# One hybrid encoder block on one core: the input projection's matmuls ordered by part, and the FFN's casts, closing tiles and stores queued anew

## The chip, the cores and the metric

The kernel runs on one core of a Trainium2 chip. The metric is the device time of one execution in microseconds (us); the value before is the median of three runs. A profile of one further execution is read beside it. TensorE (PE) multiplies, ScalarE (ACT) and VectorE (DVE) cast, add and evict, GpSimd (POOL) does small reductions and issues some of the DMAs, and SyncE (SP) issues most of the others. PEld is the row of TensorE's weight loads.

## What is computed

The input is x of 1 x 2048 x 1024 in float32. The layer, cut to what matters:

```python
h = rms_norm(x, pre_mix_g)
proj = h @ w_in                                   # 1024 -> 5376 columns
p_att, p_rwkv, p_gate = split(proj)               # 1536, 1792, 2048 columns
y_a = chunk_band_attention(q, k, v, rel_bias)     # own chunk of 64 and 8 before it
y_b = rwkv7_time_mix(p_rwkv, ...)                 # token shift, decay, delta rule over time
merged = sigmoid(ga) * (y_a @ proj_a) + sigmoid(gb) * (y_b @ proj_b)
x = x + rms_norm(merged @ w_out, post_mix_g)
hf = rms_norm(x, pre_ffn_g)
u = square(relu(hf @ w_up)) @ w_down              # 1024 -> 4096 -> 1024
x = x + rms_norm(u, post_ffn_g)
```

## The kernel before

**Precision.** Every large product is made of three matmuls. An operand is split into a high part, rounded to a short format by a cast on ACT (L78), and a low part, the rest, made by a subtraction on DVE (L79). `mm3` (L82) then adds high x high, high x low and low x high in one PSUM bank. It can go through the contraction block by block, three matmuls for each, or, with its last argument, by part: all high x high, then all high x low, and the low weights last.

**Mixing.** The 2048 tokens are worked on in four groups of 512. A group goes through `phase_rwkv`, `phase_attention` and `phase_merge`. In the first two stand 42 blocks of the input projection, each a call of `dense` (L108) for 128 columns: a load of 512 KB into `wraw` (two buffers), the cast to `whi` on ACT and the subtraction to `wlo` on DVE (two buffers each), 24 matmuls of 128x128 on 128x512 into a bank `psd` (two banks), and an eviction by whoever called. Sixteen of the blocks are gates (`gate`, L743), which ACT evicts (L747) and stores. The gates have no other dependence, and they are strewn between the steps of the RWKV recurrence (ST, L702, on DVE and PE) and of a triangular inverse that runs on DVE for some 30 us at a time (L584, L590). In the kernel before, only the first two blocks of the program multiply by part; the other 166 go by contraction block.

**The order of instructions.** Nothing of the order on an engine is fixed by the program text alone. A planner goes through the instructions with estimated costs; on each engine it places next the one that it believes ready, and among those the one that comes first in the program. On the chip each engine then works its queue strictly in the planned order. `queue_behind(a, b)` (L92) puts a into the queue after b without a semaphore, `keep_in_program_order` pins an instruction, and `place` (L96) hangs some matmuls of the recurrence behind the n-th matmul of the projection.

**FFN.** The hidden layer is worked on in two halves of 1024 tokens, with a seven-product scheme for 2x2 blocks (additions on DVE take the place of an eighth product). `phase_up` (L1226) makes the products of w_up. For each of 16 pairs of column blocks it loads two `wraw` (four buffers) and splits the combinations a1, s12, s3 and s4. The first eight (`early`) have their A11 product made ahead of the loop, so that the loop begins to load and split a1 at i = 8. The results X are squared relus, evicted by DVE and ACT (L1278 to L1280) and stored on POOL's queue to `xd`.

`phase_down` (L1347) multiplies them with w_down in 56 steps: seven products, named 1, 6, 7, 5, 4, 3, 2 in this order, of eight steps each. A step loads `xraw` and `wdraw` (L1378 to L1383), splits both into one operand tile `fop` and makes 24 matmuls; the last two steps of a product are taken together. Operands are prepared two steps ahead. After a product's last step `gather` (L1406) adds its banks to u. The closing tile of 128 tokens, `final` (L1418), loads x1 (L1422), sums squares on ACT (L1427), scales on DVE (L1428), takes the root on POOL (L1430, L125, L127), adds on DVE (L1434) and stores the output on SP's queue (L1437). The first four closing tiles stand behind product 4, the other four behind products 3 and 2.

**Beside it.** While the first half's `phase_down` runs, a generator `beside` (L1515) does work for the second half: a residual and its transposes, combinations of h on POOL's queue, and `first_half(2)` (L1217), which loads four pieces of h, casts each on ACT (L1214) and subtracts on DVE (L1215) in place.

## Time and profile before

| what | value |
|---|---|
| median of 3 runs | 3273.53 us (3273.09 to 3274.3) |
| profiled execution, its own time | 3273.41 us |
| its span, first to last instruction | 3271.7 us |
| mean granted TensorE clock | 0.996 |
| ACT busy | 1571.1 us (48%) |
| DVE busy | 2244.4 us (69%) |
| POOL busy | 592.7 us (18%) |
| one cast of 128x1024 on ACT (whi) | 1.05 us |
| one subtraction of 128x1024 on DVE (wlo) | 1.23 us |

"Idle before" in a group's row, and the bracket behind a row of the timeline, is the time that the engine stood still ahead of these instructions, with what ended it. Matmuls are pipelined: each is shown for some 0.39 us while they follow each other at shorter steps, so that a small delay can vanish in the overlap. A window's row gives a stretch, its length, each engine's busy time with the count of instructions in it, the granted clock as a share of full speed, the DMA engines' share and GB/s. A row of the timeline that ends in xN is a run of N like instructions.

### The profile page before, as it was taken

To read this page: it belongs to the slowest core of one execution; us is meant where nothing else is said; L and a number is where in the kernel's file an instruction comes from. 1 tells how busy PE (TensorE), PEld (TensorE's weight loads), DVE (VectorE), ACT (ScalarE), POOL (GpSimd) and SP (SyncE) were. 2 spreads that over 40 slices of the span, in tenths; PEclk is the share of its full clock that TensorE was granted. 3 is DMA by queue.
4 is the path that set the end of the run, shared out by engine and by line. 5 is a ranking of instruction groups with operands and counts; after the bars stand their busy time and mean duration, and the time that the engine had idled before them with its cause. 6 is when DMAs were issued, how large, how long until landed. Compare 5 with 4: busy or idle time off the path is not lost. (4 is left out here: it accounts for less than half of the span.)

```text
span 3271.7 us, 49957 instructions
## 1 busy us (share of the span) xinstructions
PE 3178.6 (97%) x18913; PEld 2591.9 (79%) x18913; DVE 2244.4 (69%) x3655; ACT 1571.1 (48%) x2511; POOL 592.7 (18%) x1093
## 2 busy tenths in 40 slices
PE   8999999999999999999999999999999999999998
PEld 6777778777878777878777877878888877888887
DVE  7785666776766775776876775777655768775465
ACT  4434634444644434644434754444543444444333
POOL 2221013122112222102222110121211112120000
PEclk9999999999999999999999999999999999999999
DMA  5245373247574237565336557654787875556565
GB/s 167 85 137 175 121 241 119 72 147 245 172 227 133 88 111 246 182 207 164 94 97 225 165 183 256 196 184 149 263 280 251 281 240 185 167 177 228 193 213 180
DMA packets 432282, 592.53 MB, mean 181 GB/s; under 512 B 25301, under 2 KB 295841, under 8 KB 432041
## 3 DMA queue, kind: packets, MB, share of 16 engines
q1 hardware_dynamic: 375080, 413.14, 40.4%
q0 software_dynamic: 47744, 159.42, 13.3%
q10 hardware_dynamic: 9216, 16.78, 1.4%
q8 instruction: 149, 2.44, 0.3%
q14 instruction: 93, 0.75, 0.1%
HBM read 425.37 MB, written 167.01 MB: 181 GB/s over the span
## 5 line engine op out<-in xcount | busy, mean ns | idle before, releaser
L1401 PE MATMUL ps_dn<-fop 128*128 128x512 f32 x2688 | 612.0, 389 | 3.6 <-DVE fop L79 3.6
L1401 PEld LDWEIGHTS ps_dn<-fop 128*128 128x128 f32 x2688 | 503.9, 188 | 109.8 <-DVE fop L79 5.5
L88 PE MATMUL psd<-hh,whi 128*128 128x512 f32 x1344 | 538.9, 403 | 11.9 <-ACT gate L747 6.8
L88 PE MATMUL psd<-hl,whi 128*128 128x512 f32 x1344 | 533.1, 398 | 0.0
L88 PE MATMUL psd<-hh,wlo 128*128 128x512 f32 x1344 | 531.2, 397 | 0.0
L78 ACT CAST whi<-wraw 128x1024 fp32r<-128x1024 f32 x232 | 243.4, 1049 | 425.6 <-PE psd L88 324.2
L79 DVE TENSOR_TENSOR wlo<-wraw,whi 128x1024 fp32r<-128x1024 f32 x232 | 284.6, 1227 | 117.5 <-ACT whi L78 117.2
L88 PEld LDWEIGHTS psd<-hh,whi 128*128 128x128 f32 x1344 | 254.0, 189 | 65.1 <-ACT gate L747 8.9
L88 PEld LDWEIGHTS psd<-hh,wlo 128*128 128x128 f32 x1344 | 252.9, 188 | 50.9 <-issue 0.7
L88 PEld LDWEIGHTS psd<-hl,whi 128*128 128x128 f32 x1344 | 253.2, 188 | 47.2
L79 DVE TENSOR_TENSOR fop<-xraw,fop 128x1024 fp32r<-128x1024 f32 x112 | 137.1, 1224 | 166.8 <-ACT fop L78 165.9
L78 ACT CAST fop<-xraw 128x1024 fp32r<-128x1024 f32 x112 | 117.8, 1052 | 245.2 <-PE ps_dn L1401 163.6
L1283 POOL DMA_DIRECT2D xd<-X x192 | 103.8, 541 | 394.3 <-ACT X L1280 339.5
L79 DVE TENSOR_TENSOR fop<-wdraw,fop 128x1024 fp32r<-128x1024 f32 x112 | 136.8, 1221 | 30.3 <-ACT fop L78 29.9
L78 ACT CAST fop<-wdraw 128x1024 fp32r<-128x1024 f32 x112 | 117.7, 1050 | 46.0 <-DMA wdraw<-in_w_down_dram 29.2
L947 DVE CUSTOM_DVE_ANT_0 sc<-bias,ps_s 128x640 f32<-128x640 f32 (+4 forms) x128 | 93.8, 733 | 57.2 <-PE ps_pt L958 32.1
L952 ACT ACTIVATE sc<-sc,mn 128x640 f32<-128x640 f32 (+4 forms) x128 | 97.7, 764 | 45.5 <-DVE mn L947 44.1
L78 ACT CAST s12h<-s 128x1024 fp32r<-128x1024 f32 x32 | 33.7, 1053 | 164.3 <-PE ps_u L88 164.3
L88 PE MATMUL ps_p<-yh,whi 128*128 128x512 f32 x256 | 101.0, 403 | 7.8 <-DVE th L1097 4.2
L963 DVE TENSOR_TENSOR PTl<-ps_pt,PTh 128x640 fp32r<-128x640 f32 (+4 forms) x128 | 94.3, 737 | 18.4 <-ACT PTh L962 16.9
L1126 PE MATMUL ps_o<-wlo,mh 128*128 128x512 f32 x256 | 100.9, 394 | 3.6 <-DVE wlo L79 3.6
L1126 PE MATMUL ps_o<-whi,mh 128*128 128x512 f32 x256 | 101.5, 396 | 0.8 <-ACT whi L78 0.8
(368 smaller groups left out, 6819.3 us busy)
## 6 DMA issues: line engine op xcount, KB each, us to landing
wraw<-in_w_in_dram SPq DMA_DIRECT2D x168, 512.0 KB
xraw<-xd SPq DMA_DIRECT2D x112, 512.0 KB
xd<-X POOLq DMA_DIRECT2D x192, 256.0 KB, 5.2
wraw<-in_w_up_dram SPq DMA_DIRECT2D x80, 512.0 KB
wdraw<-wd SPq DMA_DIRECT2D x64, 512.0 KB
wdraw<-in_w_down_dram SPq DMA_DIRECT2D x48, 512.0 KB
gd<-gate ACTq DMA_DIRECT2D x64, 256.0 KB
wd<-cmb POOLq DMA_DIRECT2D x64, 256.0 KB, 4.2
```

Source lines behind the costliest of these rows:

```text
L78: high = self.high = self.nc.scalar.copy(hi, src)
L79: self.low = self.nc.vector.tensor_tensor(lo, src, hi.bitcast(F32), ALU.subtract).ins
L88: mm.append(nc.tensor.matmul(ps, l, r, start=n == 0, stop=n == last).ins)
L947: nc.vector.tensor_tensor_reduce(sc[:, 0:n], bias[:, s0:640], pss[:, c0 : c0 + n], 1.0, 3.0e38, ALU.add, ALU.min, mn,)
L952: nc.scalar.activation(sc[:, 0:n], sc[:, 0:n], AF.Exp, scale=-1.0, bias=mn, accum_out=sm[:, col : col + 1])
L963: nc.vector.tensor_tensor(lv, pst[:, 0:nk], hv.bitcast(F32), ALU.subtract)
L1126: nc.tensor.matmul(ps[t], l[:, k, ts], r[:, k % 2], start=k == 0 and j == 0, stop=k == KB - 1 and j == 2)
L1283: nc.gpsimd.dma_start(self.xd[q][i // 2][:, i % 2], src)
L1401: nc.tensor.matmul(ps, o[:, l, k, sl], o[:, r, k], start=start and n == 0, stop=stop and n == end)
```

## The change

Every block of the input projection now multiplies by part. In the FFN, the casts of `first_half(2)` are put into ACT's queue behind the second cast of `phase_down`'s step 1. The a1 cast of iteration 8 of `phase_up`'s loop is put behind the s3 cast of iteration 7. The first four closing tiles are taken one behind each of the first four steps of product 3. In the first half, the output is stored on POOL's queue.

```diff
@@ dense
-        self.mm = self.mm3(ps, [(wh[:, k], wl[:, k], self.h[0][:, k], self.h[1][:, k]) for k in range(KB)], first)
+        self.mm = self.mm3(ps, [(wh[:, k], wl[:, k], self.h[0][:, k], self.h[1][:, k]) for k in range(KB)], True)
@@ split_here
-        self.nc.scalar.copy(hi, lo.bitcast(F32))
+        high = self.nc.scalar.copy(hi, lo.bitcast(F32))
...
+        return high.ins
@@ first_half
-            self.split_here(bh[:, ks], bl[:, ks])
+            high = self.split_here(bh[:, ks], bl[:, ks])
+            if g:
+                self.queue_behind(high, self.second)
@@ phase_up
-                self.split(*hl, src)
+                self.cast = self.split(*hl, src)
...
                 if i >= early:
+                    behind = self.cast3
                     A11, A12 = parts(raw0, "a1", KB)
+                    if i == early:
+                        self.queue_behind(self.cast, behind)
...
                 S3, A22 = parts(raw1, "s3", KB)
+                self.cast3 = self.cast
@@ phase_down
                 if s == 1:
                     self.queue_behind(self.relu, high)
+                    self.second = high
...
-                nc.sync.dma_start(self.out[g * G + ts.start : g * G + ts.stop], u[t])
+                queue = nc.sync if half else nc.gpsimd
+                queue.dma_start(self.out[g * G + ts.start : g * G + ts.stop], u[t])
...
                         gather(q, t, ps[t])
-                        if q == "4":
-                            advance(ends[GT + t])
-                        elif q == "3":
+                        if q == "3":
                             advance(ends[t], 1)
                         elif q == "2":
                             advance(ends[t])
+                if q == "3" and f < GT:
+                    advance(ends[GT + f])
```

## The prediction

> **What bounds the kernel now.** I read the page first, then TensorE's waits, then the timeline around the longest of them.

> ```profile
> span 3271.7 us, 49957 instructions
> ...
> PE 3178.6 (97%) x18913; PEld 2591.9 (79%) x18913; DVE 2244.4 (69%) x3655; ACT 1571.1 (48%) x2511; POOL 592.7 (18%) x1093
> ```
> ```profile
> PE psd L88 <- ACT gate L747: 6.8, 8, 1.2
> ...
> PE ps_u L88 <- ACT s3h L78: 4.1, 2, 2.2
> ...
> PE ps_dn L1401 <- DVE fop L79: 3.6, 4, 1.7
> ...
> PE ps_st L699 <- DVE ST L702: 2.8, 4, 0.7
> ...
> PE ps_u L88 <- DVE s3l L79: 1.0, 2, 0.5
> ```

> TensorE is busy for 97% of the span and no matmul is taken away, so the change can only win standstills: 93 us (3271.7 - 3178.6) at most. The second fence (who waited for whom: us in total, times, longest) names those that the edited lines touch. They sum to 18.3 us. A standstill costs more than its row says:

> ```profile
> 28.06 1.98 PE L88 MATMUL psd<-hl,whi 128*128 128x512 f32 x8
> ```
> ```profile
> 2567.38 32.96 PE L1401 MATMUL ps_dn<-fop 128*128 128x512 f32 x144 [1.72 <-DVE fop L79]
> ```

> In the long run 144 matmuls take 32.96 us, 0.229 each, while one is shown for some 0.39. The last one's tail is counted busy, so each separate standstill costs its idle time and another 0.16 us.

> **1. The projection by part.** The direct gain would be a wait for the low weights. There is none:

> ```profile
> L88 PE MATMUL psd<-hh,wlo 128*128 128x512 f32 x1344 | 531.2, 397 | 0.0
> ```

> The idle time before the matmuls that read wlo is 0.0 over all 168 blocks. The pace does not change either: the eight matmuls at 28.06 above are in a block that already goes by part, and (1.98 - 0.39)/7 = 0.227 us is the pace of the long run. What moves is indirect. A block can run 16 matmuls instead of two before it needs wlo, and it lets whi go 8 matmuls, 1.8 us, earlier. Where this matters, once in each group:

> ```profile
> 190.01 0.50 PE L88 MATMUL psd<-hh,whi 128*128 128x512 f32 x1 [1.17 <-ACT gate L747]
> ...
> 191.45 0.33 PE L699 MATMUL ps_st<-ST,TQ 64*64 64x64 f32 x4 [0.70 <-DVE ST L702]
> ```
> ```profile
> 188.20 1.05 ACT L78 CAST whi<-wraw 128x1024 fp32r<-128x1024 f32 x1 [1.18 <-PE psd L88]
> 189.27 0.69 ACT L747 ACTIVATE gate<-psd,hgb 128x512 f32<-128x512 f32 x1
> ```
> ```profile
> 191.42 1.21 DVE L79 TENSOR_TENSOR wlo<-wraw,whi 128x1024 fp32r<-128x1024 f32 x1
> ```
> ```profile
> 182.00:235.00 53.00, 51.08 (x320) 41.19 (x320) 47.29 (x118) 18.39 (x29) 14.67 (x23) 1.00 0.52 163
> ```

> Before 190.01 a block had put in its first two matmuls. Its wlo came only at 192.6 (191.42 + 1.21), so TensorE turned to the next block, whose bank was still to be evicted. That eviction stood on ACT behind a cast that had waited for the end of a block. By part the first block goes on with 14 more matmuls, 3.2 us, which covers both standstills: 1.17 + 0.70 + 2 x 0.16 = 2.19 us, four groups 8.8 us. I do not take all of it. DVE is busy for 47.29 of these 53 us (third number of the window's row), and the recurrence and the inverse hang on it; a TensorE that gets ahead here waits for them a little later. I take half, 4.4 us, with 0 and 8.8 as ends. A loss is possible too; it is the second rival.

> [...] The rows:

> ```profile
> L88 PEld LDWEIGHTS psd<-hh,whi 128*128 128x128 f32 x1344 | 254.0, 189 | 65.1 <-ACT gate L747 8.9
> ...
> L88 PEld LDWEIGHTS psd<-hl,whi 128*128 128x128 f32 x1344 | 253.2, 188 | 47.2
> ```

> Both neighbours have 1344 loads of their own, so nothing is shared now that could be lost. [...]

> **2. The a1 cast behind the s3 cast.**

> ```profile
> 2146.56 1.05 ACT L78 CAST a1h<-wraw 128x1024 fp32r<-128x1024 f32 x1 [4.29 <-DMA wraw<-in_w_up_dram]
> ...
> 2150.70 1.03 ACT L78 CAST s3h<-wraw 128x1024 fp32r<-128x1024 f32 x1
> ```
> ```profile
> 2151.78 0.50 PE L88 MATMUL ps_u<-t3h,s3h 128*128 128x512 f32 x1 [2.21 <-ACT s3h L78]
> ```
> ```profile
> 2777.49 0.50 PE L88 MATMUL ps_u<-t3h,s3h 128*128 128x512 f32 x1 [1.85 <-ACT s3h L78]
> ```
> ```profile
> 2153.10:2155.60 2.50, 2.50 (x6) 2.02 (x7) 2.50 (x5) 0.00 (x0) 1.57 (x3) 0.50 0.54 148
> 2778.80:2781.30 2.50, 2.50 (x11) 2.08 (x12) 2.50 (x5) 0.00 (x0) 1.57 (x3) 1.00 0.56 152
> ```

> The a1 cast of iteration 8 stands 4.29 us on its load, and two pairs of relus, s4h and s3h stand behind it; TensorE then waits for s3h and, 1 us later, for s3l. With s3h first, ACT has 4.29 us in which to make it, more than the 2.21 by which it is late. The a1 cast that is moved is wanted four products later, 48 x 0.229 = 11 us, and its own load has landed by 2146.56, so nothing queued behind it is late next. Gain: idle time 2.21 + 1.85, s3l's two waits 1.0 in all, 4 x 0.16 for the tails, 5.7 us. In the first half the standstill is followed by a clock of 0.50 (third number from the end), in the second by 1.00: 6 matmuls in 2.5 us against 11, so 5 x 0.229 = 1.2 us more. Sum 6.9.

> [...] Here 2.21 us, followed by another short wait, was enough in one half and 1.85 was not in the other; I go by the first.

> **3. The casts of first_half(2) behind step 1's.**

> ```profile
> 2323.19 1.05 ACT L1214 CAST bh<-bl 128x1024 fp32r<-128x1024 f32 x1 [3.74 <-DMA bl<-ht]
> ...
> 2332.74 1.04 ACT L78 CAST fop<-xraw 128x1024 fp32r<-128x1024 f32 x1
> ```
> ```profile
> 2337.69 11.18 PE L1401 MATMUL ps_dn<-fop 128*128 128x512 f32 x48 [1.10 <-DVE fop L79]
> 2349.49 2.83 PE L1401 MATMUL ps_dn<-fop 128*128 128x512 f32 x11 [0.62 <-DVE fop L79]
> ```

> The four casts and their subtractions now run ahead of step 1's operands, which TensorE then awaits for 1.10 us; 1.26 with the tail. Moved behind, they are 4 x 1.05 on ACT and 4 x 1.2 on DVE between the operands of steps 1 and 2. Step 1's 5.5 us (24 x 0.229) of matmuls cover most of that. The second wait (0.78 with tail) hangs on a late load and may go or grow. I take 1.3, ends -1 and 2.0.

> **4. Closing tiles and stores, first half.**

> ```profile
> 2566.22 0.34 SPq L1437 DMA_DIRECT2D out_dram<-u  x1
> ```
> ```profile
> 2567.64 1.05 ACT L78 CAST fop<-xraw 128x1024 fp32r<-128x1024 f32 x1 [5.10 <-DMA xraw<-xd]
> ```
> ```profile
> 2557.36 1.29 DVE L1428 TENSOR_TENSOR u<-u,g_post 128x512 f32<-128x512 f32 x2
> ...
> 2559.71 1.41 DVE L1434 SCALAR_TENSOR_TENSOR u<-u,rs_r,x1r 128x512 f32<-128x512 f32 x2 [1.06 <-DMA x1r<-x]
> ```

> Four closing tiles come at once behind product 4, each with its store on SP's queue; a store waits there for DVE, and the operand loads wait behind it. ACT stands 5.10 us for one of them and TensorE 1.72 (the x144 row above). With the tiles spread over four steps and the stores on POOL, this 1.88 goes. Each step then carries 1.29 + 1.41 us of closing on DVE beside two subtractions of 1.2, 5.1 of 5.5 us: close, but prepared two steps ahead. In the second half, where the store stays on SP, one tile per step holds the loads for less time than four at once. At the end of the first half:

> ```profile
> 2644.99 6.45 SPq L1437 DMA_DIRECT2D out_dram<-u  x3
> ```
> ```profile
> 2653.34 0.99 SPq L1256 DMA_DIRECT2D t2l<-td  x2
> ```
> ```profile
> 2659.08 1.05 ACT L1214 CAST t2h<-t2l 128x1024 fp32r<-128x1024 f32 x1 [2.87 <-DMA t2l<-td]
> ```
> ```profile
> 2661.18 0.50 PE L88 MATMUL ps_u<-bh,a1h 128*128 128x512 f32 x1 [0.99 <-ACT z L1300]
> ```

> Three stores hold SP until 2651.4; then come the loads of t2, a cast that stands 2.87 us for one of them, and the eviction z behind the cast, for which TensorE waits 0.99. Without the stores the loads go out earlier: 1.2 us with the tail, ends 0 and 1.2. On POOL the stores wait in the same way, and POOL's roots for the next tile and the first xd stores of the new half queue behind them; nobody on TensorE's path waits for these.

> **Sum.** 4.4 + 6.9 + 1.3 + 1.9 + 1.2 = 15.7. Against it I set one new standstill of 0.78, the size of the one at 2349.49, somewhere among what is moved: 14.9. The profiled execution took 3273.4 us by its own time, 1.7 more than its span and 0.1 less than the median of the runs. 3273.4 - 14.9 = 3258.5; with the 0.1, I say 3259.

> **Rivals.** *The projection gives nothing.* DVE at 47.29 of 53 us takes the 4.4 back, and parts 3 and 4 get only half of theirs: 6.9 + 2.2 - 0.8 = 8.3, 3265. If DVE falls behind in product 3 too, it is about 3268. For it speaks that row; against it, that TensorE's two standstills there are real.

> *Slower: a cast ahead of an eviction.* whi comes free 1.8 us earlier, so the planner can put the next cast further ahead in ACT's queue, in front of an eviction; if its load has not landed, the eviction stands behind it, as at 2146.56. That case cost 2.21 + 0.16 + 1.2 on TensorE, 3.6 us. Twice in each group is 28.6 us, less 10.5 from the FFN (parts 2 to 4 and the new standstill): 3292. It decides from a load that lands after the block's sixteenth matmul. Against it: at 188.20 the cast waited for TensorE, not for its load.

> *Larger.* All 8.8 and both ends of part 3 and 4 come: 8.8 + 6.9 + 2.0 + 1.9 + 1.2 = 20.8, 3253; a stall or two more that vanish with the reordering, each of 2.19, 3249.

> *The edits do not bind.* The planner goes by readiness, so closing tiles may still come early and part 4 (3.1) be lost: 3262.

> [...]

> **How the numbers follow.** Forecast, with the case of edits that do not bind, 0.60; larger 0.16; nothing from the projection 0.17; slower 0.06; shared loads 0.01. A measurement of this kernel can tell 0.2% from no change, 6.5 us: faster is below 3267.0. The forecast, the larger case and a third of the third make 0.60 + 0.16 + 0.06 = 0.82 faster; the rest of the third, 0.11, is the same; 0.07 slower. The range goes from 3248, the larger case, to 3268, the poor end of the third.

> **What would show it.** The waits for ACT gate (6.8) fall to about 2 and for s3h (4.1) to 0; the window after iteration 7 has a clock of 1.00; the casts of L1214 stand behind 2333, and the wait at step 1 is gone; no closing tile stands before product 3; SP issues t2l before 2648. A new wait of psd for an eviction, or a longer ps_t wait for DVE in each group, would make the first term wrong, and with four groups that decides the sign.

## The result, and the profile after

| | us | runs |
|---|---|---|
| before | 3274.57 (3267.09 to 3279.44) | 20 |
| changed | 3267.51 (3260.27 to 3272.55) | 20 |
| ratio | 0.9976, 95% interval 0.9969 to 0.9982 | |

The ratio makes 7.9 us, faster by a little more than the 0.2% that can be told from no change, and about half of the 14.9 us forecast. The profiled execution took 3272.55 us and is the slowest of the 20, so its parts are read with care. Its page, the span and the engines' busy time:

```profile
span 3270.8 us, 50026 instructions
...
PE 3184.3 (97%) x18913; PEld 2599.2 (79%) x18913; DVE 2239.5 (68%) x3655; ACT 1576.9 (48%) x2511; POOL 596.0 (18%) x1101
```

As many matmuls as before keep TensorE busy for 5.7 us longer (3184.3 against 3178.6). Two rows of the timeline split each execution, the FFN's first matmul (start, duration) and its last run. Before, then changed:

```profile
2019.38 0.39 PE L88 MATMUL ps_u<-bh,a1h 128*128 128x512 f32 x1
...
3259.24 1.29 PE L1401 MATMUL ps_dn<-fop 128*128 128x512 f32 x5
```
```profile
2027.89 0.39 PE L88 MATMUL ps_u<-bh,a1h 128*128 128x512 f32 x1
...
3258.83 0.84 PE L1409 MATMUL ps_dn<-fop 128*128 128x512 f32 x3
```

From the first to the end of the second are 1241.2 us before and 1231.8 changed: the FFN won 9.4 us. The mixing in front of it took 8.5 longer in this pair of executions; how much of that the order of instructions makes is seen under the experiments. TensorE's waits in the changed kernel (who waited for whom: us in total, times, longest) say with whom. ST is the recurrence, X, Z and XT belong to the inverse, yt is the transpose of the recurrence's result, QA, KK, mn and PTl are tiles of attention and th one of the merge:

```profile
PE psd L88 <- DVE QA L894: 10.7, 4, 2.9
PE ps_at L643 <- ACT XT L628: 9.4, 4, 2.4
PE ps_t L615 <- DVE X L593: 6.8, 5, 1.7
...
PE ps_st L699 <- DVE ST L702: 5.1, 4, 1.3
...
PE ps_t L623 <- ACT Z L618: 4.7, 8, 0.8
PE ps_u L88 <- ACT z L1303: 2.3, 3, 1.5
...
PE ps_dn L1409 <- DVE fop L79: 1.7, 3, 0.8
```

The waits for gate (6.8 us before) and for s3h and s3l (4.1 and 1.0) are no longer in the view. ST did not go but grew, from 2.8 to 5.1, and QA, XT and the inverse (X, Z) came up: QA had 2.6 us before, and the wait at 144.00 for XT was 1.13 us. All idle time between TensorE's first matmul and the FFN's first, summed over the rows of the trace, is 61.3 us before and 61.4 changed (the expectations count 66 and 67, with the same outcome). So by part did not lower that sum. It took many short standstills (104 of more than 0.1 us in the whole trace, 86 changed) and left fewer, longer ones. Of those longer than 1.8 us behind the program's start and ahead of the FFN, there are three before (2.55, 2.25 and 1.91 us) and ten changed: XT and QA in each of the four groups, one for th (2.54) and one for o (1.81).

The standstill at 143.10 cost more than its length. Behind it, the windows (stretch, busy time and count of each engine, granted clock third from the end):

```profile
144.60:148.00 3.40, 3.40 (x27) 2.44 (x24) 1.06 (x1) 1.17 (x2) 0.36 (x1) 0.50 0.00 0
148.50:152.00 3.50, 3.50 (x56) 2.83 (x52) 0.79 (x3) 2.00 (x6) 0.00 (x0) 1.00 0.52 150
```

In the first TensorE is busy throughout at half clock. The trace of the kernel before has five such stretches ahead of its last microseconds, 17.1 us in all, four of them in the mixing; the changed one has ten, 37.5 us, all in the mixing.

**Where the two longest come from.** At XT, ACT's timeline and then TensorE's:

```profile
139.72 0.62 ACT L78 CAST rh<-r 128x512 fp32r<-128x512 f32 x1 [1.73 <-DVE r L496]
140.37 0.69 ACT L364 ACTIVATE r<-psd,omu 128x512 f32<-128x512 f32 x1
140.95 1.03 ACT L78 CAST whi<-wraw 128x1024 fp32r<-128x1024 f32 x1
141.88 1.16 ACT L628 COPY XT<-ps_t 32x512 f32<-32x512 f32 x2
```
```profile
143.10 0.66 PE L643 MATMUL ps_at<-ident,AR 128*128 128x128 f32 x4 [2.35 <-ACT XT L628]
```

XT's copies empty the bank that the next transposes need. The weight cast, 1.03 us, now stands in front of them; in the kernel before a weight cast stood ahead of Z, and these copies came straight behind r. At the start of attention, ACT, DVE, then TensorE:

```profile
301.18 1.05 ACT L78 CAST whi<-wraw 128x1024 fp32r<-128x1024 f32 x1 [2.43 <-PE psd L88]
302.26 0.59 ACT L891 ACTIVATE QA<-psd 64x512 fp32r<-64x512 f32 x1
```
```profile
303.05 1.22 DVE L79 TENSOR_TENSOR wlo<-wraw,whi 128x1024 fp32r<-128x1024 f32 x1 [2.09 <-ACT whi L78]
304.31 0.69 DVE L894 SCALAR_TENSOR_TENSOR QB<-psd,QA 64x512 fp32r<-64x512 f32 x1
```
```profile
305.85 3.75 PE L88 MATMUL psd<-hh,whi 128*128 128x512 f32 x8 [2.90 <-DVE QA L894]
```

The cast waits 2.43 us for TensorE to let go of a whi buffer, the eviction QA of an older block stands behind it, and so does DVE's half of that eviction behind wlo. The next block has no bank until both are done.

### The profile page after: what moved, and what is told of

Read it like the earlier page. It is cut to its first block, busy times and chain, and to the rows that moved or that the text cites. A ratio compares the mean times of both kernels' runs of the same rounds, so it can differ in the third digit from the quotient of the medians.

```text
span 3270.8 us, 50026 instructions
## 1 busy us (share of the span) xinstructions
PE 3184.3 (97%) x18913; PEld 2599.2 (79%) x18913; DVE 2239.5 (68%) x3655; ACT 1576.9 (48%) x2511; POOL 596.0 (18%) x1101
## 5 line engine op out<-in xcount | busy, mean ns | idle before, releaser
L78 ACT CAST whi<-wraw 128x1024 fp32r<-128x1024 f32 x232 | 243.5, 1050 | 392.9 <-PE psd L88 301.1
L88 PE MATMUL psd<-hh,whi 128*128 128x512 f32 x1344 | 370.3, 403 | 10.7 <-DVE QA L894 10.7
L79 DVE TENSOR_TENSOR wlo<-wraw,whi 128x1024 fp32r<-128x1024 f32 x232 | 283.0, 1220 | 133.3 <-ACT whi L78 70.0
L88 PE MATMUL psd<-hl,whi 128*128 128x512 f32 x1344 | 367.2, 401 | 0.0
L88 PE MATMUL psd<-hh,wlo 128*128 128x512 f32 x1344 | 358.4, 398 | 0.0
L88 PEld LDWEIGHTS psd<-hh,whi 128*128 128x128 f32 x1344 | 244.8, 190 | 59.8 <-issue 11.8
L88 PEld LDWEIGHTS psd<-hl,whi 128*128 128x128 f32 x1344 | 249.1, 190 | 49.5
L88 PEld LDWEIGHTS psd<-hh,wlo 128*128 128x128 f32 x1344 | 247.9, 189 | 50.8 <-issue 1.4
L79 DVE TENSOR_TENSOR fop<-xraw,fop 128x1024 fp32r<-128x1024 f32 x112 | 137.0, 1224 | 178.9 <-ACT fop L78 178.7
L78 ACT CAST fop<-xraw 128x1024 fp32r<-128x1024 f32 x112 | 117.8, 1052 | 256.4 <-PE ps_dn L1409 186.3
L79 DVE TENSOR_TENSOR fop<-wdraw,fop 128x1024 fp32r<-128x1024 f32 x112 | 136.6, 1220 | 19.0 <-ACT fop L78 18.8
L78 ACT CAST fop<-wdraw 128x1024 fp32r<-128x1024 f32 x112 | 117.7, 1051 | 34.8 <-DMA wdraw<-in_w_down_dram 20.0
L78 ACT CAST s12h<-s 128x1024 fp32r<-128x1024 f32 x32 | 33.7, 1053 | 163.0 <-PE ps_u L88 163.0
L88 PE MATMUL ps_p<-yh,whi 128*128 128x512 f32 x256 | 102.6, 405 | 6.0 <-DVE th L1097 5.3
L962 ACT CAST PTh<-ps_pt 128x640 fp32r<-128x640 f32 (+4 forms) x128 | 79.7, 623 | 55.2 <-PE ps_pt L958 54.6
```

The lines of the kernel that those rows point to most:

```text
L78: high = self.high = self.nc.scalar.copy(hi, src)
L79: self.low = self.nc.vector.tensor_tensor(lo, src, hi.bitcast(F32), ALU.subtract).ins
L88: mm.append(nc.tensor.matmul(ps, l, r, start=n == 0, stop=n == last).ins)
L962: nc.scalar.copy(hv, pst[:, 0:nk])
```

## The experiments

All ratios are to the kernel before, on the same chip.

**By part alone, FFN edits alone.** The four pieces of the change:

```diff
# e1: only
+        ... for k in range(KB)], True)
# e2: everything else; e3: only the a1 cast
+                    if i == early:
+                        self.queue_behind(self.cast, behind)
# e4: first_half's casts, closing tiles and stores
```

By part alone: 

> Only the projection by part; the FFN is that of the kernel before. Theory A (half clock): by part joins TensorE's short standstills into fewer, longer ones of about the same sum (66 us before, 67 after in the mixing of the two profiles), and a window of half clock follows more of them; slower than before by 3 to 8 us, with 7 or more windows of half clock ahead of the FFN against 4. Rival B (the prediction's first term): faster by 4.4 us. Rival C (profile of after was an unlucky execution): within 2 us of before, with 4 to 6 windows.

All FFN edits: 

> All edits of the FFN, the projection as before. Theory A: the FFN's whole gain is left, 9 to 12 us faster than before, faster than the changed kernel by 3 to 5. Rival B: 10.5 us faster than before, slower than the changed kernel by 4.4 were the first term right; with the changed kernel at 7 faster, the FFN would then have brought only 2.6. Rival C: 7 us faster, equal to the changed kernel.

The a1 cast alone: 

> Only the a1 cast behind the s3 cast. The prediction's part 2: 6.9 us faster, 5.7 if the half clock after iteration 7 had nothing to do with the standstill; no wait for s3h in the up stage of either half. Rival: the standstill moves to a1 or s12 of iteration 8 and half of it comes back, 3 us faster.

The other three FFN edits: 

> The FFN's other three edits without the a1 cast: casts of first_half(2), closing tiles, stores. The prediction's parts 3 and 4 with the new standstill: 1.3 + 1.9 + 1.2 - 0.8 = 3.6 us faster. Rival, from the profile of after, where TensorE waits 1.46 for z at the start of the second half (0.99 before) and 0.57 to 0.77 twice in the first steps of the down stage: about 1 us faster, since only the wait in product 3 is gone.

| kernel | ratio, 95% | us by the ratio |
|---|---|---|
| by part alone | 1.0008 (0.9999 to 1.0017) | +2.6 |
| FFN edits | 0.9970 (0.9956 to 0.9983) | -9.8 |
| a1 cast alone | 0.9964 (0.9951 to 0.9978) | -11.8 |
| the other FFN edits | 0.9994 (0.9985 to 1.0003) | -2.0 |

By part alone gains nothing; a loss of up to 5.6 us lies in its interval. The 2.6 us are a little under the 3 to 8 of its theory A, and seven stretches of half clock stand ahead of the FFN, as that theory asked. The a1 cast carries the FFN's gain, and nothing measurable is added by the other three.

These traces also say how the pair of profiles is to be read. Ahead of the FFN, the kernel with by part alone has the same sequence of instructions on TensorE, ACT and DVE as the changed kernel, and the three kernels with FFN edits have that of the kernel before. Yet the FFN's first matmul came at 2018.8 us with by part alone and at 2027.9 in the changed kernel, and at 2019.4, 2020.3, 2010.4 and 2021.0 in the kernel before and those three. One order scatters by some 10 us from execution to execution, with eleven and seven windows of half clock there in the first two, and four, four, one and five in the others. So most of the 8.5 us of the pair belongs to its two executions.

What lasts over the runs is the mean granted clock: 0.9937 in the eleven runs with by part alone, 0.9957 in the 22 runs of the kernel before. A clock lower by 0.0020 is 6.5 us of work in an execution of 3271 us. Against it stand 2.2 us less of idle time ahead of the FFN (59.0 against 61.3) and 18 standstills fewer, each with a tail of 0.16, 2.9 us. The rest, a loss of 1.4 us, lies within the interval of the 2.6 measured; this is an estimate from those figures.

**By part in the RWKV phase only.** Attention's blocks as before, everything else as changed.

```diff
-        ... for k in range(KB)], True)
+        ... for k in range(KB)], first or self.by_part)
...
+            self.by_part = False
             for p in range(NP):
                 self.att_pair(g, p, beside)
+            self.by_part = True
```

> The changed kernel, but only the blocks of the RWKV phase go by part; the 12 blocks of attention in each group go by contraction block as before. Theory (most of what by part loses is the wait for QA at the start of attention): psd's wait for QA goes back from 10.7 to about 2.6 us, and the time falls by some 8 us, to 3258 to 3262. Rival (the loss is made in the RWKV phase, by the waits for XT and for the inverse): the time stays within 3 us of 3267.5.

The ratio is 0.9977 (0.9969 to 0.9986), the same as the changed kernel's. The wait for QA did fall, to 3.5 us, but waits that by part had removed in attention came back (5.8 us for mn, 4.0 for PTl). The rival holds so far as the time goes: by part in attention gives with one hand what it takes with the other.

**QA's eviction ahead of the next cast.** An edit on the changed kernel:

```diff
         ps = self.dense(ATT0 + p * P)
+        if p:
+            self.queue_behind(self.high.ins, self.q_act)
+            self.queue_behind(self.low, self.q_dve)
...
+            self.q_act = nc.scalar.activation(QB[ow, par], ps[rw], AF.Copy, scale=-0.125).ins
...
+                self.q_dve = nc.vector.scalar_tensor_tensor(
```

> The changed kernel, with one edit: at the start of attention, the cast and the subtraction of the next pair's first weights are queued behind the evictions of the pair before (QA, QB). Theory (by part lets whi go earlier, so the planner puts that cast and subtraction in front of an eviction; that wait is new, real and not hidden): psd's wait for QA falls from 10.7 us to 3 or less, no window of half clock follows it, and the time falls by 8 to 12 us against the changed kernel, to 3256 to 3260. Rival (the evictions of K, next on the same engines, are late instead): the wait moves on to KK, and the time stays within 3 us of 3267.5.

0.9955 (0.9942 to 0.9967), some 7 us better than the changed kernel (0.9969 to 0.9982), a little under what was expected. TensorE at the same place:

```profile
303.58 2.06 PE L88 MATMUL psd<-hh,whi 128*128 128x512 f32 x8 [0.68 <-ACT KK L903]
```

The 2.90 us are 0.68, now for KK as the rival had it, and behind them eight matmuls take 2.06 us instead of 3.75. The waits for QA and KK together are 1.4 us in this trace.

**The transposes behind XT placed later.**

```diff
+                mm = nc.tensor.transpose(...)
+                if p == 0 and h == 1 and j == 0:
+                    self.place(mm, 437)
```

> The changed kernel, with one edit: the first transposes ps_at that wait for XT's copy are placed 8 matmuls of the projection later (behind number 437 of the group). Theory (the standstill is a matter of order; the projection has work for it): the wait of ps_at for XT falls from 9.4 us to 2 or less, the windows of half clock at 145, 626 and 1640 us are gone, and the time falls by 8 to 12 us, to 3256 to 3260. Rival (the recurrence hangs on these transposes, so it is late by as much): the waits of ps_st for ST grow from 5.1 us to 12 or more and the time stays within 3 us of 3267.5.

0.9954 (0.9941 to 0.9968), again some 7 us. XT's wait at 143.65 is 0.30 us, and no half clock follows there. The recurrence does not pay for it, as this kernel's waits show, but a part reappears one step later (yt, which the changed kernel's view did not have):

```profile
PE ps_yt L729 <- ACT yf L734: 5.8, 4, 1.8
PE ps_t L615 <- DVE X L593: 5.5, 6, 1.8
...
PE ps_st L701 <- DVE ST L704: 4.3, 4, 1.1
```

**All three standstills.** The two edits above, and the second inverse's groups 8 matmuls later:

```diff
-BLOCKS = ((412, 424), (623, 632))
+BLOCKS = ((412, 424), (631, 640))
```

> The changed kernel with three edits: the order of QA's evictions, the later place of the transposes behind XT, and in the same manner the second inverse's two groups of 32x32 matmuls placed 8 projection matmuls later (numbers 631 and 640 in place of 623 and 632). Theory (the three standstills are separate, and each had work that could fill it): the waits for QA, XT and X are down to 3 us or less each; the first two edits brought 0.21% and 0.22% alone and add up, the third brings 4 x 1.65 us and up to four windows of half clock: a ratio to the kernel before of 0.990 to 0.992 (some 3240 to 3247 us). Rival (DVE's recurrence and inverse take the time back): the waits for ST, X and th grow, and the ratio stays at 0.9945 or more.

0.9897 (0.9884 to 0.9911), a little past what its theory asked for: 3239.17 us beside 3273.34 before, the fastest version of the study. Its page and waits:

```profile
span 3238.3 us, 50028 instructions
...
PE 3171.3 (98%) x18913; PEld 2590.4 (80%) x18913; DVE 2240.6 (69%) x3655; ACT 1575.9 (49%) x2511; POOL 602.4 (19%) x1101
```
```profile
PE ps_yt L729 <- ACT yf L734: 8.3, 4, 2.8
PE ps_pv L974 <- ACT PTh L967: 4.5, 11, 0.6
PE ps_st L701 <- DVE ST L704: 4.3, 4, 1.1
```

QA and X are gone from the head of the list and XT is down to 1.2 us. Idle time in front of the FFN, counted as above, is 42.2 us, 19 less than in the changed kernel, and two stretches of half clock are left there. The mean clock of its four runs is 0.9980.

**The same, but by contraction block.**

```diff
-        ... for k in range(KB)], True)
+        ... for k in range(KB)], first)
```

> The same kernel with all edits, but the projection goes by contraction block as before. Theory (by part itself is worth the 3 to 4 us of the prediction, and lost them to the longer standstills and the windows behind them): its ratio lies 0.0005 to 0.002 above that of the kernel with the three edits. Rival (by part itself is worth nothing or costs): the ratios agree within 0.0005, or this one is the faster.

0.9964 (0.9951 to 0.9978), 0.0067 above the by-part twin, some 22 us and far more than either theory gave. Idle time in front of the FFN is 56.9 us against 42.2, made of many short waits: 6.0 us for Z, 6.0 for mn, 4.0 for th. The places 437, 631 and 640 were chosen for by part, so this is the worth of by part in that order, not in every order. Beside the kernel with the FFN edits alone (0.9970), the three edits bring nothing measurable by contraction block. It is by part and the places together that win.

**The third edit alone.**

> The changed kernel with the third edit alone: the second inverse's two groups of 32x32 matmuls 8 projection matmuls later (631 and 640 in place of 623 and 632). The three edits together brought 0.79% against the changed kernel (ratios 0.9976 and 0.9897), the first two alone 0.21% and 0.22%, so 0.36%, 12 us, is left for this one. Theory (the gains add): the waits for X and Z fall from 11.5 us to 5 or less, no half clock follows the second inverse, and the ratio is 0.993 to 0.995. Rival (the three gains help one another: alone, the matmuls spent here are missing at the standstills behind, which grow): the ratio is 0.9955 or more.

0.9984 (0.9974 to 0.9995), not better than the changed kernel, as its rival had it. The wait for X fell from 6.8 to 0.7 us, but Z behind it grew from 4.7 to 6.2, and half clock still follows twice (243 and 1226 us; four times in the changed kernel). The three gains do not add: alone, the third is worth nothing, and some 12 us are left for it on top of the other two if those two add, which no run shows. Idle time does nearly add (11.2, 5.6 and 4.0 us less alone, 19.2 together), time does not. The mean clock of the twelve runs fits that: at 0.9938 it is no higher than the changed kernel's 0.9948, while all three edits have 0.9980. Why the clock did not recover stays open: counted by the standstills of its trace, in the way of the last section, this kernel should have fewer windows of half clock (8.8 against 11.0).

**z ahead of the t2 cast.** On the kernel with the three edits, in the second half:

```diff
+            if half:
+                self.queue_behind(highs[0], zs[2])
```

> The kernel with the three edits and one more: in the second half's phase_up, the first cast of t2 is queued behind the third eviction z. Theory (the wait for z at the start of the second half comes from that cast, which stands in front of z for a load, and not from the stores): the standstill of 1.5 us there is gone, and the time is 1 to 3 us lower than with the three edits. Rival (the load itself is late for everything): the wait goes to t2h or t2l, and the time is the same within 0.7 us.

0.9910 (0.9896 to 0.9923), not better. The 1.56 us at z are gone, and a longer standstill has come instead:

```profile
2637.50 0.80 PE L88 MATMUL ps_u<-bh,a1h 128*128 128x512 f32 x1 [3.05 <-DVE x L1288]
```
```profile
2632.24 1.22 DVE L1220 TENSOR_TENSOR t2l<-t2l,t2h 128x1024 fp32r<-128x1024 f32 x1 [3.83 <-ACT t2h L1219]
...
2636.76 0.68 DVE L1288 TENSOR_TENSOR x<-z,ps_u 128x512 f32<-128x512 f32 x1
```

DVE's eviction x now stands behind the subtractions of t2 and t3, which wait for the same loads and casts. The late load of t2 is paid for elsewhere, near to what the rival had, though the wait went to x and not to t2h or t2l.

**Standstills by themselves.** This kernel computes nothing of the layer. Every matmul is tied behind the one before, and a chain of copies on ACT makes the standstills. It ran once.

```diff
+                for r in range(1, 7):
+                    for n in (128, 320, 512):
+                        t = self.stand(ps, r, n)
...
+                        self.put(nc.tensor.matmul(p2[:, 0:128], self.w, t[:, 0:128], start=True, stop=True))
+                        ps = self.dense(52 + 3 * (rep % 3), self.x)
```

> A kernel that computes nothing of the layer: TensorE runs dense stretches of 52 to 58 matmuls of 128x128 on 128x512, and between them it stands still for 18 lengths from about 0.5 to 4 us, 7 times each; then 24 pairs of standstills of about 0.9 us with 4 matmuls between; then 24 stretches of 96 or 160 matmuls of 32x32 without a standstill. Theory (the clock is set by a fixed grid of 3.413 us, and a window of it in which TensorE stands for more than about 1.7 us is followed by a window of half clock): all half windows begin on one grid; standstills under 1.7 us are never followed by one, of 2.0 us in about 0.56 of cases, of 2.4 us in 0.67, of 3.0 us in 0.85, from 3.5 us always; a pair of 0.9 us counts by its sum where both fall in one window. Rival (the length of the one standstill decides): a sharp bound near 2 us, above which all are followed by half clock and below which none, and pairs never. [...]

Two standstills of the same 1.84 us, and the windows over each and behind it (clock third from the end):

```profile
1045.08 0.33 PE L101 MATMUL ps_dense<-link,wh 128*128 128x128 f32 x1 [1.84 <-ACT link L75]
...
1315.86 0.33 PE L101 MATMUL ps_dense<-link,wh 128*128 128x128 f32 x1 [1.84 <-ACT link L75]
```
```profile
1043.00:1046.40 3.40, 1.56 (x8) 1.16 (x7) 1.59 (x6) 0.00 (x0) 1.00 0.00 0
1046.50:1049.90 3.40, 3.40 (x17) 2.82 (x16) 0.00 (x0) 0.00 (x0) 1.00 0.00 0
1313.20:1316.50 3.30, 1.46 (x7) 0.95 (x6) 1.59 (x6) 0.00 (x0) 1.00 0.00 0
1316.60:1320.00 3.40, 3.40 (x10) 2.63 (x9) 0.00 (x0) 0.00 (x0) 0.50 0.00 0
```

The second was followed by half clock and 10 matmuls in 3.4 us, the first by full clock and 17. What differs is where they fall. All half windows of this trace begin at the same remainder of 3413.33 ns, within 5 ns, over 2.7 ms. Of seven standstills of 1.84 us four were followed by one, of seven of 2.34 us two, of seven of 2.80 us five, of seven of 3.14 us seven; none of a single one under 1.8 us. Cut along that grid, the largest idle part that a single standstill put into one window without half clock behind it is 1.83 us, the smallest with it 1.84. The rival falls: of standstills of one length, 1.84 us, some were followed by half clock and some were not. The theory's grid holds in this trace, with 1.83 us where it had 1.7. Pairs of 0.73 us with four matmuls between were followed by half clock eight times in 24, which neither the sum of their idle times (1.46) nor one of them explains alone; their tails and the narrow matmul between, not in the idle column, may make up the rest, which is not shown.

## Why the prediction was half right

The FFN was forecast to win 10.5 us and won 9.4 in the pair of profiles, 9.8 by the FFN edits alone. The projection was forecast at -4.4 and came out at +2.6 alone. That one term is nearly all of the missing 7 us. The rival "The projection gives nothing" (8.3 us won) is the one that came true: 3267.51 lies at the poor end of the range, which that rival had set. That the FFN's sum came out is in part luck. Parts 3 and 4 with the new standstill were to bring 3.6 us; their edits alone brought 2.0 by the runs and 1.6 in the FFN of their trace (1239.6 us), and the a1 cast more than its 6.9.

**1. The projection by part: the failing step.** "By part the first block goes on with 14 more matmuls, 3.2 us, which covers both standstills" held for the first: the wait for gate went from 6.8 us to none. It failed for ST, 0.70 us at 191.45 before and 1.29 at 192.63 changed. What failed is the step from a standstill that is covered to time that is won: the 8.8 us, halved or not, did not leave the sum of idle time (61.3 and 61.4), they moved. And the loss that the text called possible came from two sides. DVE takes its part back, as the first rival had it: TensorE reaches the second inverse earlier and waits 1.65 us for X in each group. The second rival's mechanism, a weight cast in front of an eviction, came too, at QA and XT. At QA it decided not from a late load but from a whi buffer that TensorE still held (2.43 us at 301.18); at XT the cast waited for nothing, and its own 1.03 us stood in front. What the prediction did not see is that waits of the same sum cost more here in larger pieces, 37.5 us at half clock ahead of the last microseconds against 17.1. Before, one standstill for gate was 1.17 us in each group, and longer ones came singly (2.55 for KK at 302.42); changed, XT's is 2.35 and QA's 2.6 to 2.9 in every group, past the 1.83 us of the kernel of standstills. The edits that remove them show that it is a matter of order: with QA's or XT's put right the by-part kernel is some 7 us ahead of the changed one, and with all three 26 us ((0.9976 - 0.9897) x 3273). How these 26 us divide among the three is not shown. The 0.01 for shared loads came to nothing: each of the two rows of whi has 1344 weight loads before and changed (254.0 and 253.2 us before, 244.8 and 249.1 changed).

**2. The a1 cast.** Right. ACT, iteration 7 in the changed kernel:

```profile
2155.43 1.06 ACT L78 CAST s3h<-wraw 128x1024 fp32r<-128x1024 f32 x1
```

No idle time stands ahead of it and no wait for s3h behind it; the clock in the window 2156.5 to 2159 is 1.00, as forecast. Alone the edit's FFN took 1233.6 us, 7.5 less than before (6.9 forecast). The 7.5 hold 1.57 us of part 4's wait as well, and 1.4 us more of waits in the down stage's first steps, so the near agreement is in part luck. The 11.8 us of its runs are more than that stage shows; its interval reaches from 7 to 16. The term took its reading of the clock from one pair of standstills: "Here 2.21 us, followed by another short wait, was enough in one half and 1.85 was not in the other; I go by the first". The runs do not bear it out. With by part alone, a shorter wait for s3h in the second half (1.51 us) was followed by half clock (at 2776.8); in the kernel before 1.85 was not.

**3. The casts of first_half(2).** The wait at step 1 went, as forecast, and two later ones took its place:

```profile
2352.81 5.73 PE L1409 MATMUL ps_dn<-fop 128*128 128x512 f32 x24 [0.77 <-DVE fop L79]
2359.11 5.51 PE L1409 MATMUL ps_dn<-fop 128*128 128x512 f32 x23 [0.57 <-DVE fop L79]
```
```profile
2347.71 1.05 ACT L78 CAST fop<-xraw 128x1024 fp32r<-128x1024 f32 x1 [4.14 <-DMA xraw<-xd]
...
2350.45 1.05 ACT L78 CAST fop<-wdraw 128x1024 fp32r<-128x1024 f32 x1 [1.69 <-DMA wdraw<-in_w_down_dram]
```

1.34 us against 1.72 before: worth about 0.4, not 1.3. In the kernel without the a1 cast it is 1.77 (1.00 and 0.77), worth nothing. ACT waits for loads there, so the order of casts does not bind. Together with the 0.78 set against the sum as one new standstill, the forecast here comes to 0.5, which is about right.

**4. Closing tiles and stores.** The wait of 1.72 us ahead of product 3 is gone, but it is gone as well in the kernel with the a1 cast alone, which keeps the closing tiles where they were (0.15 us is left there). It cannot be booked to this edit. The term for z failed outright: it was forecast to go and grew from 0.99 to 1.46 us. SP's queue and the wait in the changed kernel:

```profile
2654.94 0.38 SPq L1270 DMA_DIRECT2D wraw<-in_w_up_dram  x1
2655.42 1.13 SPq L1259 DMA_DIRECT2D t2l<-td  x2
```
```profile
2663.75 0.50 PE L88 MATMUL ps_u<-bh,a1h 128*128 128x512 f32 x1 [1.46 <-ACT z L1303]
```

The stores have left SP, and t2l goes out at 2655.42 all the same, not "before 2648". In front of it stands a load of weights, which waits for a buffer that s3l frees at about 2654.9 (DVE at 2653.69, 1.22 us). It did so before too (2652.84); the stores that ended at 2651.4 were not what was waited for last.

## What to carry to other kernels

An edit that lets TensorE run further ahead of its helpers does not lower their debt. Follow it to the next place where it must wait, and look there for a cast or a load that now stands in front of an eviction. Do not price standstills by their sum: the four waits for XT of 1.09 to 1.13 us in the kernel before had no half clock behind them, and three of the four of 2.33 to 2.36 us in the changed one did. And by part was worth nothing in one order and some 22 us in another, where work was placed at the long ones. One profile of each kernel is not enough to price such an edit: the same order of the mixing differed by some 10 us between two executions.

## What the hardware showed

**Stretches of 32x32 matmuls with half clock behind them.** In the kernel of standstills, TensorE without any idle time, in 32x32 matmuls alone, from the start of such a stretch:

```profile
2286.20:2289.30 3.10, 3.10 (x100) 3.10 (x100) 0.00 (x0) 0.00 (x0) 1.00 0.00 0
2289.40:2292.80 3.40, 3.40 (x69) 3.40 (x67) 0.00 (x0) 0.00 (x0) 0.50 0.02 5
```

It is busy all the time, and its clock goes from 1.00 to 0.50. So it fits that the 64 small matmuls of the inverse (runs of 0.24 and 1.19 us) beside waits of 0.82 and 0.36 us for Z are followed by half clock (at 243.6 in the changed kernel), where windows of the same trace with 1.41 to 1.70 us of waiting alone are not.
